# An encoder kernel's attention: one reciprocal for the first three row blocks of a head, and the last q blocks' rotation in other rounds

## The chip, the core and the metric

The kernel runs on one core of a Trainium2 chip. The core has five engines that each run their own list of instructions in order: TensorE (PE, matrix products; its weight loads are shown apart as PEld), VectorE (DVE), ScalarE (ACT), GpSimd (POOL) and SyncE (SP, which issues most transfers). An instruction that waits for another engine holds up everything behind it on its own engine. The metric is the device time of one execution in microseconds (us). Three runs of the kernel before gave 1718.39, 1720.16 and 1721.22 us, a median of 1720.16 us.

## The reference, cut to what matters

Two sequences of 512 tokens go through two layers. Layer 0 mixes tokens by a Fourier transform, layer 1 by attention; each is followed by a squared-ReLU MLP. The change is in the attention of layer 1: 8 query heads of 128, two key/value heads, a softmax over 512 keys.

```python
q = rms_norm(q, q_gain); k = rms_norm(k, k_gain)
q = axial_rope(q, ang_row, ang_col) * (HEAD_DIM ** -0.5)
k = axial_rope(k, ang_row, ang_col)
s = jnp.einsum("bqkgd,bskd->bkgqs", q_blk, k)
p = jax.nn.softmax(s, axis=-1)
o = jnp.einsum("bkgqs,bskd->bqkgd", p, v)
```

## The kernel before, in words

Every float32 operand is split into a rounded high half and a remainder, and a product is made of three matmuls (`mm3`, lines 77, 78 and 79: high by high, high by low, low by high). A split (`split`, lines 82 and 83) is a cast on ACT and then a subtraction on DVE.

The attention has 2 x 8 = 16 heads, one after the other. A head has four row blocks of 128 queries. For each, `scores` makes a 128x512 block of scores on PE, its row maximum on DVE (line 1476), the exponential with a row sum on ACT (line 1478), the reciprocal of the sum on DVE (line 1479) and the scaling of the block by it on POOL (line 1480). `transpose_p` turns a block of 128 keys of all four row blocks with four PE transposes (line 1486), so its fourth transpose needs the head's fourth scaled block. `transpose_q` does the same for q (line 1465). `values` makes the product with v.

The loop at line 1556 runs a pipeline; one pass of it is called round n here. Round n makes the scores of head n, block by block, each followed by a set of four transposes of head n-1's probabilities; then the transposes of head n+1's q; then the values of head n-1. On PE the first block of scores of the next round stands behind the values. All of this goes through a scheduler that sets the order of each engine's list when the kernel is built, from its own costs; buffers are given out in that order too: eight temporary blocks of 128x512 (tag t2) and eight PSUM banks. So a change in the code moves rows on every engine.

The query blocks of the second sequence's last two row blocks (of heads 4 to 7) are not rotated before the loop. A generator, `norm_rope`, is called one step at a time in the loop at line 1562. Its first step makes the inverse norms, with a square root on ACT, which needs another function table than the exponential. Each of its next four steps rotates one pair of heads: two scalings on ACT (line 1434), one product on POOL (line 1440), two on DVE (line 1443), one sum on POOL (line 1445). Before, the five steps stand in rounds 3, 4, 5, 6 and 7. The blocks are first needed at the end of round 11.

Two more lines are used below: line 1417 (four sums of squares on ACT, in round 0 and 2, for these norms) and line 1571 (the loads of w_o, whose splits the scheduler puts into rounds 0 and 1, lines 82 and 83 with `w` and `raw`).

Of the kernel before, what the change touches and what calls it, by code (L numbers as in the profile page):

```python
# [14 lines left out]
AF = mybir.ActivationFunctionType  # L15
ALU = mybir.AluOpType
# [6 lines left out]
NT = S // P  # L23
# [17 lines left out]
def trunk_kernel(ctx, tc, x_in, xt_in, y_out, dcos, dsin, feat, rope, gfour, gcol, grow, gfin,  # L41
                 w_four, w_nyq, w_qkv, w_o, w_up, w_row2, w_row4, w_sum2, w_sum4, w_down):
    nc = tc.nc
# [13 lines left out]
    def nm(s):  # L57
        n_[0] += 1
        return f"{s}_{n_[0]}"

    def slot(shape, dt):
        return act.tile(shape, dt, tag="u4", name=nm("u"))

    def tm(shape=(P, 512), dt=F32):
        return tmp.tile(list(shape), dt, tag="t2", name=nm("t"))

    def small(n=4):
        return sm.tile([P, n], F32, tag="s", name=nm("s"), padded_shape=[P, 8])

    def ps():  # L70
        return psp.tile([P, 512], F32, tag="ps", name=nm("ps"))
# [4 lines left out]
    def mm3(out, lh, ll, rh, rl, first, last):  # L76
        nc.tensor.matmul(out, lh, rh, start=first, stop=False)  # L77
        nc.tensor.matmul(out, lh, rl, start=False, stop=False)  # L78
        nc.tensor.matmul(out, ll, rh, start=False, stop=last)  # L79

    def split(dst_hi, dst_lo, src, eng=nc.vector):
        nc.scalar.copy(dst_hi, src)  # L82
        eng.tensor_sub(dst_lo, src, f32(dst_hi))  # L83
# [26 lines left out]
    def load_w(src, eng=nc.vector, parts=1, home=own):  # L110
        raw = load_raw(src)
        w = home()
        for i in range(parts):
            sl = slice(i * 1024 // parts, (i + 1) * 1024 // parts)
            split(w[0][:, sl], w[1][:, sl], raw[:, sl], eng)
        return w
# [1278 lines left out]
    for which, sc in (("q", HD ** -0.5), ("k", 1.0)):  # L1395
        r = slot([P, 2, NT, HD], F32)
# [7 lines left out]
    def qkv(cg, q, t, ws, k0=0, k1=KC, o=None):  # L1404
        o = ps() if o is None else o
        cols = slice(t * P, (t + 1) * P)
        for k in range(k0, k1):
            w = ws[k // 2]
            c = (k % 2) * 512
            mm3(o, hT[q][k][:, 0, cols], hT[q][k][:, 1, cols],  # L1410
                w[0][:, c : c + 512], w[1][:, c : c + 512], k == 0, k == KC - 1)
        return o

    def head_squares(raw, h0, n, ss):
        junk = tm((P, n * HD), BF16)
        for h in range(h0, h0 + n):
            nc.scalar.activation(junk[:, (h - h0) * HD : (h - h0 + 1) * HD], raw[:, h * HD : (h + 1) * HD],
                                 AF.Square, accum_out=ss[:, h : h + 1])
# [42 lines left out]
    def transpose_q(q, h):  # L1461
        pt = ps()
        c = (h % 2) * HD
        for t in range(NT):
            nc.tensor.transpose(pt[:, t * P : (t + 1) * P], qr[q, h // 2][:, t, c : c + HD], ident)
        qT = slot([P, 2, 512], F32R)
        split(qT[:, 0], qT[:, 1], pt)
        return qT

    def scores(q, h, qT, t):  # L1470
        kk = kT[q, h // 4]
        s = ps()
        cols = slice(t * P, (t + 1) * P)
        mm3(s, qT[:, 0, cols], qT[:, 1, cols], kk[:, 0], kk[:, 1], True, True)
        m, sm_ = small(1), small(1)
        nc.vector.tensor_reduce(m[:, :1], s, AX.X, ALU.max, negate=True)
        p = tm()
        nc.scalar.activation(p, s, AF.Exp, bias=m[:, :1], accum_out=sm_[:, :1])
        nc.vector.reciprocal(sm_[:, :1], sm_[:, :1])
        nc.gpsimd.tensor_scalar(p, p, sm_[:, :1], 1.0, ALU.mult, ALU.mult)  # L1480
        return p

    def transpose_p(probs, sc):
        pt = ps()
        for t in range(NT):
            nc.tensor.transpose(pt[:, t * P : (t + 1) * P], probs[t][:, sc * P : (sc + 1) * P], ident)
        k = slot([P, 2, 512], F32R)
        split(k[:, 0], k[:, 1], pt)
        return k

    def values(q, h, pts):
        o = ps()
        c = (h // 4) * HD
        for sc in range(NT):
            vh, vl = vt[q][0][:, sc, c : c + HD], vt[q][1][:, sc, c : c + HD]
            mm3(o, vh, vl, pts[sc][:, 0], pts[sc][:, 1], sc == 0, sc == NT - 1)
        t = slot([P, 2, 512], F32R)
        split(t[:, 0], t[:, 1], o)
        oT[q, h] = t
# [7 lines left out]
    for cg in (2, 0, 1):  # L1507
        ws = wkv if cg == 2 else [load_w(w_qkv[cg, u], home=own if u < 2 else lent) for u in range(4)]
        for q in range(NSEQ):
# [6 lines left out]
            for t in range(NT if (cg, q) != (1, 1) else 2):  # L1516
                if (cg, q, t) in transposes:
                    transpose_k(transposes[cg, q, t])
                if (cg, q, t) == (1, 1, 1):
                    first = transpose_q(0, 0)  # L1520
# [9 lines left out]
                r = rs[q][:, t : t + 1]  # L1530
# [13 lines left out]
    heads = [(q, h) for q in range(NSEQ) for h in range(NH)]  # L1544
    raw, ss = slot([P, 1024], F32), small(8)
    o = qkv(1, 1, 2, ws)
    probs = [scores(*heads[0], first, t) for t in range(NT)]
    nc.scalar.activation(raw[:, :512], o, AF.Copy, scale=rs[1][:, 2:3])
    head_squares(raw, 0, 4, ss)
    qT = transpose_q(*heads[1])  # L1550
# [5 lines left out]
    for n in range(1, len(heads) + 1):  # L1556
        pts, nxt = [], []
        for t in range(NT):
            if n < len(heads):
                nxt.append(scores(*heads[n], qT, t))  # L1560
            pts.append(transpose_p(probs, t))
            if n > 2 and t == 0:
                next(todo, None)
        last = nxt[-1] if nxt else last
        if n + 1 < len(heads):
            qT = transpose_q(*heads[n + 1])
        values(*heads[n - 1], pts)
        if n == 2:
            head_squares(raw, 4, 4, ss)
        probs = nxt  # L1570
        if n in (6, 8, 10, 12):
            ahead.append(load_w(w_o[len(ahead)], nc.vector, 2))
# [294 lines left out]
```

## Time and profile before

| | |
|---|---|
| median of three runs | 1720.16 us |
| the profiled execution | 1717.6 us, of which the span is 1715.8 us |
| PE busy | 99% of the span, granted clock 0.997 |
| DVE, ACT, POOL busy | 72%, 50%, 20% |
| the attention's rounds | from 853 to 985 us of the span |

A row of the timeline reads: start in us, duration in us, engine, line, operation, output tile <- input tiles, shape, count; in brackets how long the engine was idle before it, and what ended that. Matmuls overlap in the pipeline, so a matmul shows 0.39 us though the next starts 0.23 us later; a PE that is 99% busy can still lose time, and it is seen best in the distance between equal places of two rounds.

### The profile page before, as it was taken

Reading aid. Unit: us, or ns where it says so; the run is one execution under the profiler, and the core shown is the slowest. Engines: PE = TensorE matmul, PEld = TensorE weight load, DVE = VectorE, ACT = ScalarE, POOL = GpSimd, SP = SyncE. Lnnn points to the kernel's source line nnn. Section 1 sums busy time; section 2 is a strip of 40 time slices with the busy share of each in tenths; the row PEclk is TensorE's granted clock in tenths of the full one; section 3 lists DMA queues with packets and bytes.
Section 4 is the critical chain, followed back from the end, with each engine's and each line's share of the span. In section 5 each row is a group of like instructions: output and inputs, shape, how many; then the busy total and the mean of one; then the engine's idle time right before and its main releaser. Section 6 shows DMA issues by size and latency. Waiting matters only on the chain. (4 is left out here: it accounts for less than half of the span.)

```text
span 1715.8 us, 21892 instructions
## 1 busy us (share of the span) xinstructions
PE 1691.0 (99%) x7847; PEld 1395.8 (81%) x7847; DVE 1239.0 (72%) x1836; ACT 857.8 (50%) x1508; POOL 335.5 (20%) x302
## 2 busy tenths in 40 slices
PE   9999999999999999999999999999999999999997
PEld 6988887888788888888877888788788888888886
DVE  8679776456887879976588834687655479787865
ACT  6666445446343434457687714554444544344334
POOL 1321442321000000232244303114422200000004
PEclk9999999999999999999999999999999999999999
DMA  9742554449554645610000213335534686455322
GB/s 322 191 143 95 196 202 163 161 172 367 197 197 138 214 148 175 232 42 28 26 25 1 99 50 123 110 114 197 181 142 148 225 303 237 163 204 193 115 74 99
DMA packets 103679, 266.33 MB, mean 155 GB/s; under 512 B 10177, under 2 KB 10177, under 8 KB 103570
## 3 DMA queue, kind: packets, MB, share of 16 engines
q1 hardware_dynamic: 87410, 232.95, 38.4%
q10 hardware_dynamic: 14112, 25.70, 4.0%
q0 software_dynamic: 2048, 6.29, 1.8%
q8 instruction: 61, 1.00, 0.2%
q14 instruction: 48, 0.39, 0.1%
HBM read 189.93 MB, written 73.92 MB: 154 GB/s over the span
## 5 line engine op out<-in xcount | busy, mean ns | idle before, releaser
L833 PE MATMUL ps<-u,w 128*128 128x512 f32 x4656 | 1068.9, 390 | 5.3 <-DVE w L83 1.2
L833 PEld LDWEIGHTS ps<-u,w 128*128 128x128 f32 x4656 | 873.4, 188 | 192.3 <-DVE w L83 2.7
L82 ACT CAST w<-raw 128x1024 fp32r<-128x1024 f32 (+1 forms) x224 | 217.6, 981 | 435.8 <-PE ps L833 266.6
L83 DVE TENSOR_TENSOR w<-raw,w 128x1024 fp32r<-128x1024 f32 (+1 forms) x224 | 258.0, 1154 | 71.9 <-ACT w L82 71.5
L159 POOL TENSOR_TENSOR t<-t,t 128x512 f32<-128x512 f32 (+1 forms) x56 | 79.0, 1410 | 738.1 <-ACT t L157 682.0
L83 DVE TENSOR_TENSOR u<-u,u 128x1024 fp32r<-128x1024 f32 x132 | 157.6, 1220 | 25.8 <-ACT u L82 25.2
L82 ACT CAST u<-u 128x1024 fp32r<-128x1024 f32 x132 | 132.4, 1044 | 70.5 <-PE ps L833 48.5
L77 PE MATMUL ps<-u,u 128*128 128x512 f32 (+2 forms) x388 | 150.0, 388 | 1.9 <-DVE u L496 1.4
L1089 DVE TENSOR_TENSOR u<-ps,u 128x512 f32<-128x512 f32 x160 | 109.4, 686 | 53.9 <-PE ps L833 53.3
L78 PE MATMUL ps<-u,u 128*128 128x512 f32 (+2 forms) x388 | 144.8, 373 | 1.4 <-DVE u L83 1.4
L79 PE MATMUL ps<-u,u 128*128 128x512 f32 (+2 forms) x388 | 144.5, 372 | 0.0
L833 PE MATMUL ps<-u,u 128*128 128x512 f32 x576 | 138.2, 391 | 2.4 <-DVE t L924 2.3
L833 PEld LDWEIGHTS ps<-u,u 128*128 128x128 f32 x576 | 107.6, 188 | 27.1 <-DVE t L924 2.6
L950 POOL TENSOR_TENSOR u<-u 128x512 f32<-128x512 f32 x28 | 36.6, 1305 | 411.3 <-ACT u L849 411.3
L83 DVE TENSOR_TENSOR u<-ps,u 128x512 fp32r<-128x512 f32 (+4 forms) x118 | 74.6, 650 | 17.4 <-ACT u L82 16.2
L78 PEld LDWEIGHTS ps<-u,u 128*128 128x128 f32 x388 | 73.4, 189 | 14.1 <-DVE u L83 3.9
L77 PEld LDWEIGHTS ps<-u,u 128*128 128x128 f32 x388 | 73.5, 190 | 13.8 <-DVE u L496 1.6
L79 PEld LDWEIGHTS ps<-u,u 128*128 128x128 f32 x388 | 73.1, 188 | 13.0 <-DVE u L83 0.4
L911 DVE TENSOR_TENSOR t<-ps,u 128x512 f32<-128x512 f32 x30 | 20.7, 690 | 81.8 <-PE ps L833 63.8
L82 ACT CAST u<-ps 128x512 fp32r<-128x512 f32 (+4 forms) x118 | 64.6, 562 | 28.8 <-PE ps L79 10.9
L816 DVE TENSOR_TENSOR u<-ps,u 128x512 f32<-128x512 f32 (+1 forms) x48 | 30.8, 644 | 64.8 <-PE ps L79 64.8
L77 PE MATMUL ps<-u,w 128*128 128x512 f32 (+2 forms) x192 | 64.9, 338 | 0.0
(237 smaller groups left out, 2005.8 us busy)
## 6 DMA issues: line engine op xcount, KB each, us to landing
raw<-w_up SPq DMA_DIRECT2D x82, 512.0 KB, 4.5
u<-spill_t SPq DMA_DIRECT2D x60, 512.0 KB, 6.1
raw<-w_sum SPq DMA_DIRECT2D x56, 512.0 KB, 4.0
u<-spill_b SPq DMA_DIRECT2D x45, 512.0 KB, 5.2
spill_t<-u SPq DMA_DIRECT2D x87, 256.0 KB, 2.0
spill_b<-t ACTq DMA_DIRECT2D x60, 256.0 KB, 3.2
raw<-w_row SPq DMA_DIRECT2D x28, 512.0 KB, 4.1
park<-u SPq DMA_DIRECT2D x24, 512.0 KB, 3.3
```

What stands on the lines that cost most here:

```text
L77: nc.tensor.matmul(out, lh, rh, start=first, stop=False)
L78: nc.tensor.matmul(out, lh, rl, start=False, stop=False)
L79: nc.tensor.matmul(out, ll, rh, start=False, stop=last)
L82: nc.scalar.copy(dst_hi, src)
L83: eng.tensor_sub(dst_lo, src, f32(dst_hi))
L159: nc.gpsimd.tensor_add(acc[q][:, :n], acc[q][:, :n], s[:, :n])
L816: nc.vector.tensor_add(x[:, :n], o[:, :n], x[:, :n])
L833: nc.tensor.matmul(o, w[x][:, sl], h[k][y], start=first and k + i == 0, stop=k == n - 1 and i == 2, skip_group_check=not first)
L911: nc.vector.tensor_add(u2, ob, t[:, 0])
L950: eng.tensor_sub(t[:, 0], b12, b11)
L1089: nc.vector.tensor_add(x, o, x)
```

## The change

`scores` gets a list. The four row sums of a head now lie in the four columns of one small tile. Nothing is done with them after the first and the second block. After the third block one reciprocal over three columns is made, and the three scalings on POOL follow it; after the fourth block come a reciprocal of the last column and the fourth scaling. A head has two reciprocals instead of four, 32 fewer in all, and still four scalings. The generator is now called in rounds 3, 5, 7, 8 and 9.

```diff
-    def scores(q, h, qT, t):
+    def scores(q, h, qT, t, out):
...
-        m, sm_ = small(1), small(1)
+        m = small(1)
+        if t == 0:
+            out.append(small(NT))
+        r = out[0]
         nc.vector.tensor_reduce(m[:, :1], s, AX.X, ALU.max, negate=True)
         p = tm()
-        nc.scalar.activation(p, s, AF.Exp, bias=m[:, :1], accum_out=sm_[:, :1])
-        nc.vector.reciprocal(sm_[:, :1], sm_[:, :1])
-        nc.gpsimd.tensor_scalar(p, p, sm_[:, :1], 1.0, ALU.mult, ALU.mult)
-        return p
+        nc.scalar.activation(p, s, AF.Exp, bias=m[:, :1], accum_out=r[:, t : t + 1])
+        out.append(p)
+        if t > 1:
+            new = range(0, 3) if t == 2 else range(3, 4)
+            nc.vector.reciprocal(r[:, new.start : new.stop], r[:, new.start : new.stop])
+            for u in new:
+                nc.gpsimd.tensor_scalar(out[u + 1], out[u + 1], r[:, u : u + 1], 1.0, ALU.mult, ALU.mult)
...
-    probs = [scores(*heads[0], first, t) for t in range(NT)]
+    probs = []
+    for t in range(NT):
+        scores(*heads[0], first, t, probs)
...
-                nxt.append(scores(*heads[n], qT, t))
-            pts.append(transpose_p(probs, t))
-            if n > 2 and t == 0:
+                scores(*heads[n], qT, t, nxt)
+            pts.append(transpose_p(probs[1:], t))
+            if n in (3, 5, 7, 8, 9) and t == 0:
                 next(todo, None)
```

In the changed kernel the lines have other numbers: the row maximum is line 1479, the exponential 1481, the reciprocal 1485, the scaling 1487, the transposes of the probabilities 1492.

The first place is DVE's list in a round with a rotation (round 6 before, round 5 of the change), from the first row maximum on. `s` is a small tile, `ps` a PSUM bank, `u` a split block, `t` a temporary block; L83 is the subtraction of a split. Before:

```order
L1476 TENSOR_REDUCE s_1411_8039<-ps_1410_8035 128x1
L83 TENSOR_TENSOR u_1409_8032<-ps_1408_8019,u_1409_8032 128x512
L83 TENSOR_TENSOR u_1415_8051<-ps_1414_8046,u_1415_8051 128x512
L1479 RECIPROCAL s_1412_8040<-s_1412_8040 128x1
L1476 TENSOR_REDUCE s_1420_8067<-ps_1419_8063 128x1
L1443 TENSOR_TENSOR t_1418_8056<-t_1416_8054,u_913_6000 128x2x64 x2
L83 TENSOR_TENSOR u_1424_8079<-ps_1423_8074,u_1424_8079 128x512
L1476 TENSOR_REDUCE s_1426_8086<-ps_1425_8082 128x1
L1479 RECIPROCAL s_1421_8068<-s_1421_8068 128x1
L83 TENSOR_TENSOR u_1430_8098<-ps_1429_8093,u_1430_8098 128x512
L1476 TENSOR_REDUCE s_1432_8105<-ps_1431_8101 128x1
L1479 RECIPROCAL s_1427_8087<-s_1427_8087 128x1
```

And in the change:

```order
L1479 TENSOR_REDUCE s_1362_7896<-ps_1361_7892 128x1
L83 TENSOR_TENSOR u_1366_7906<-ps_1365_7901,u_1366_7906 128x512
L1479 TENSOR_REDUCE s_1371_7922<-ps_1370_7918 128x1
L1479 TENSOR_REDUCE s_1376_7938<-ps_1375_7934 128x1
L1443 TENSOR_TENSOR t_1369_7911<-t_1367_7909,u_913_6000 128x2x64 x2
L83 TENSOR_TENSOR u_1374_7931<-ps_1373_7926,u_1374_7931 128x512
L83 TENSOR_TENSOR u_1379_7951<-ps_1378_7946,u_1379_7951 128x512
L1479 TENSOR_REDUCE s_1381_7958<-ps_1380_7954 128x1
L1485 RECIPROCAL s_1363_7897<-s_1363_7897 128x3
L83 TENSOR_TENSOR u_1384_7969<-ps_1383_7964,u_1384_7969 128x512
L83 TENSOR_TENSOR u_1386_7977<-ps_1385_7972,u_1386_7977 128x512
L1485 RECIPROCAL s_1363_7897<-s_1363_7897 128x1
```

Before, the first reciprocal stands fourth; now the one for three columns stands behind all four row maxima, both rotation products and three subtractions, and the fourth column's two subtractions behind that.

The second place is DVE's list at the end of round 3, behind the last step of the inverse norms (L137). The row maxima are those of head 3's last three blocks and of head 4's first (ps_1348_7817 before, ps_1336_7797 in the change). Before:

```order
L1476 TENSOR_REDUCE s_1327_7740<-ps_1326_7736 128x1
L83 TENSOR_TENSOR u_1345_7798<-ps_1344_7793,u_1345_7798 128x512
L1476 TENSOR_REDUCE s_1333_7759<-ps_1332_7755 128x1
L1476 TENSOR_REDUCE s_1339_7778<-ps_1338_7774 128x1
L1479 RECIPROCAL s_1328_7741<-s_1328_7741 128x1
L1479 RECIPROCAL s_1334_7760<-s_1334_7760 128x1
L1476 TENSOR_REDUCE s_1349_7821<-ps_1348_7817 128x1
L83 TENSOR_TENSOR u_1347_7814<-ps_1346_7801,u_1347_7814 128x512
L1479 RECIPROCAL s_1340_7779<-s_1340_7779 128x1
```

And in the change:

```order
L1479 TENSOR_REDUCE s_1318_7723<-ps_1317_7719 128x1
L1479 TENSOR_REDUCE s_1323_7739<-ps_1322_7735 128x1
L1479 TENSOR_REDUCE s_1328_7759<-ps_1327_7755 128x1
L83 TENSOR_TENSOR u_1333_7778<-ps_1332_7773,u_1333_7778 128x512
L1479 TENSOR_REDUCE s_1337_7801<-ps_1336_7797 128x1
L1485 RECIPROCAL s_1308_7695<-s_1308_7695 128x3
L1485 RECIPROCAL s_1308_7695<-s_1308_7695 128x1
```

The remainder of head 4's q (the L83 row) has moved behind all three maxima, and the first three columns' reciprocal stands behind the first row maximum of the next head. Before, the first block's reciprocal came ahead of this whole piece; now head 3's first block is scaled with the others.

The third place is ACT's list in round 0, from the load of the exponential's table on. CAST u is the high half of a split of head 1's q (u_1256_7471 before, u_1253_7466 in the change) or of transposed probabilities, CAST w that of w_o. Before:

```order
L1478 ACT_TABLE_LOAD
L1478 ACTIVATE t_1241_7423,s_1240_7421<-ps_1238_7416,s_1239_7420 128x512
L1478 ACTIVATE t_1245_7434,s_1244_7432<-ps_1242_7427,s_1243_7431 128x512
L82 CAST u_1256_7471<-ps_1255_7466 128x512
L1478 ACTIVATE t_1249_7445,s_1248_7443<-ps_1246_7438,s_1247_7442 128x512
L82 CAST w_1561_8569<-raw_1560_8567 128x512
L1478 ACTIVATE t_1253_7456,s_1252_7454<-ps_1250_7449,s_1251_7453 128x512
L1417 ACTIVATE t_1254_7461,s_1236_7390<-u_1235_7389 128x128 x4
```

And in the change:

```order
L1481 ACT_TABLE_LOAD
L1481 ACTIVATE t_1241_7423,s_1240_7421<-ps_1238_7416,s_1239_7420 128x512
L1481 ACTIVATE t_1244_7431,s_1240_7421<-ps_1242_7425,s_1243_7429 128x512
L1481 ACTIVATE t_1247_7439,s_1240_7421<-ps_1245_7433,s_1246_7437 128x512
L1481 ACTIVATE t_1250_7451,s_1240_7421<-ps_1248_7445,s_1249_7449 128x512
L1417 ACTIVATE t_1251_7456,s_1236_7390<-u_1235_7389 128x128 x4
L82 CAST u_1253_7466<-ps_1252_7461 128x512
L82 CAST w_1528_8514<-raw_1527_8512 128x512 x2
L1560 ACTIVATE u_1235_7389<-ps_1254_7469,rs_978_6293 128x512
L82 CAST w_1580_8711<-raw_1579_8709 128x512
L82 CAST u_1260_7509<-ps_1259_7504 128x512
L82 CAST w_1580_8711<-raw_1579_8709 128x512
```

The cast of head 1's q has moved from behind two exponentials to behind four and the four sums of squares.

SP's list is the same, transfer for transfer. POOL's list has the same number of rows; in a rotated round the rotation's product and sum now stand ahead of all four scalings of that head, where before one scaling stood ahead of them.

## The prediction

> **What bounds the kernel now.** I read the page's busy times first, then the waits of the attention's stretch (853 to 990 us), then the timeline of each engine there. First the page, and from the waits the largest group that names the code of the change:
>
> ```profile
> PE 1691.0 (99%) x7847; PEld 1395.8 (81%) x7847; DVE 1239.0 (72%) x1836; ACT 857.8 (50%) x1508; POOL 335.5 (20%) x302
> ```
>
> ```profile
> PEld ps L1486 <- POOL t L1480: 3.1, 8, 1.1
> ```
>
> TensorE is the bound. In 137 us its queue waited 3.1 us, eight times, for a scaled block (at most 1.1 us at once). All that the change can win is such waiting. The timeline shows it best in the transposes of q, one set at the end of each round:
>
> ```profile
> 864.60 0.60 PE L1465 MATMUL ps<-ident,u 128*128 128x128 f32 x4
> ...
> 873.26 0.60 PE L1465 MATMUL ps<-ident,u 128*128 128x128 f32 x4
> ...
> 880.97 0.60 PE L1465 MATMUL ps<-ident,u 128*128 128x128 f32 x4
> ...
> 889.51 0.60 PE L1465 MATMUL ps<-ident,u 128*128 128x128 f32 x4
> ...
> 898.88 0.60 PE L1465 MATMUL ps<-ident,u 128*128 128x128 f32 x4
> ...
> 924.17 0.60 PE L1465 MATMUL ps<-ident,u 128*128 128x128 f32 x4
> ```
>
> The first four are the ends of rounds 1 to 4. Round 3 takes 880.97 - 873.26 = 7.71 us, and later rounds without rotation take the same: PE's own work. Over it, round 2 loses 8.66 - 7.71 = .95, round 4 .83, round 5 1.66, and rounds 6 to 8 (898.88 to 924.17, three rounds) 25.29 - 23.13 = 2.16. With .96 at the entry (below) and .4 behind the last round this is about 6.95 us, the most that could be won (.4%).
>
> **The change part by part.** A clean round first (round 11, no rotation):
>
> ```profile
> 936.51 0.68 DVE L1476 TENSOR_REDUCE s<-ps 128x1 f32<-128x512 f32 x1
> ...
> 941.10 0.17 DVE L1479 RECIPROCAL s<-s 128x1 f32<-128x1 f32 x1
> ```
>
> ```profile
> 942.69 0.69 POOL L1480 TENSOR_SCALAR t<-t,s 128x512 f32<-128x512 f32 x1 [0.56 <-DVE s L1479]
> ```
>
> ```profile
> 943.48 0.60 PE L1486 MATMUL ps<-ident,t 128*128 128x128 f32 x4
> ```
>
> Let T be the start of a round's first set of probability transposes; the next set of the next round starts at T + 7.71, here 943.48, so T = 935.77. Of the four transposes in .60 us the last starts .34 in (an estimate from the row), so the fourth scaled block is wanted at T + 8.05. It is ready at 942.69 + .69 = 943.38 = T + 7.61: .44 us to spare. With the change three scalings come in a row behind the third reciprocal. Moving up the row maxima as the changed order does, I get that reciprocal at T + 4.39 by DVE's spacings (.6 for a maximum or a subtraction, the first maximum at T + .74) and the fourth block at T + 7.5. So a clean round pays nothing: PE's 7.71 us hide it. The 32 removed reciprocals are hidden by the same cover.
>
> *The spacings in a rotated round.*
>
> ```profile
> 905.45 0.16 DVE L1479 RECIPROCAL s<-s 128x1 f32<-128x1 f32 x1
> 905.53 0.67 DVE L1476 TENSOR_REDUCE s<-ps 128x1 f32<-128x512 f32 x1
> 906.11 1.17 DVE L1443 TENSOR_TENSOR t<-t,u 128x128 f32<-128x128 f32 x2
> 907.20 0.68 DVE L83 TENSOR_TENSOR u<-ps,u 128x512 fp32r<-128x512 f32 x1
> 907.80 0.67 DVE L1476 TENSOR_REDUCE s<-ps 128x1 f32<-128x512 f32 x1
> ...
> 911.10 0.15 DVE L1479 RECIPROCAL s<-s 128x1 f32<-128x1 f32 x1
> ```
>
> ```profile
> 911.41 0.70 POOL L1480 TENSOR_SCALAR t<-t,s 128x512 f32<-128x512 f32 x1 [0.64 <-PE ps L79]
> ```
>
> From start to start a reciprocal costs DVE .08 us, a maximum or subtraction .6, the two rotation products 1.09. From a reciprocal's start to its scaling's start it is .31. The changed list of such a round (shown above) then runs: maximum T + .74, subtraction 1.34, maxima 1.94 and 2.54, products 3.14, subtractions 4.23 and 4.83, maximum 5.43, reciprocal of three columns 6.03. Four scalings of .69 follow: 6.03 + .31 + 2.76 + .05 = T + 9.15, where T + 8.05 is wanted: **1.1 us late**. Before, the first scaling stood ahead of the products and the others came one by one.
>
> Rounds 6 to 8 hold two rotations in place of three: 1.1 + 0 + 1.1 - 2.16 = **+.04**. Round 5 loses its rotation: **-1.66**. Rounds 9 and 10 were clean and now follow the rotations of rounds 8 and 9; the delayed round before shifts the lanes by about .1, so 1.0 each, **+2.0**.
>
> *Entry (rounds 0 and 1).*
>
> ```profile
> 855.92 0.69 ACT L1478 ACTIVATE t<-ps,s 128x512 f32<-128x512 f32 x1 [0.22 <-DVE s L1476]
> ...
> 857.26 0.58 ACT L82 CAST u<-ps 128x512 fp32r<-128x512 f32 x1
> ...
> 858.07 0.68 DVE L83 TENSOR_TENSOR u<-ps,u 128x512 fp32r<-128x512 f32 x1
> ...
> 859.52 0.39 PE L79 MATMUL ps<-u,u 128*128 128x512 f32 x1
> ...
> 859.58 0.33 ACT L1417 ACTIVATE t<-u 128x128 bf16<-128x128 f32 x1
> ...
> 859.75 0.49 PE L1486 MATMUL ps<-ident,t 128*128 128x128 f32 x3
> ...
> 860.75 0.62 ACT L82 CAST w<-raw 128x512 fp32r<-128x512 f32 x1
> ...
> 861.05 0.33 PE L1486 MATMUL ps<-ident,t 128*128 128x128 f32 x1 [0.82 <-POOL t L1480]
> ...
> 861.14 0.48 PE L77 MATMUL ps<-u,u 128*128 128x512 f32 x1
> ```
>
> PE's fourth transpose would follow its three at 859.75 + .34 = 860.09 and came at 861.05: .96 lost. Now ACT makes four exponentials from 855.92 (.68 apart: 858.64), the four sums of squares (860.75 - 859.58 = 1.17: 859.81) and only then head 1's q cast. Its subtraction starts .81 behind the cast's start (858.07 - 857.26) and lasts .6: 861.2, where L79, which wants it, ran at 859.52. Behind that L79 PE needs 861.14 - 859.52 - .96 = .66 us to the next L77: 861.85 against 861.14, **+.7**. The wait for the scaling is gone; the q split is late in its place.
>
> *Rounds 1 and 2.*
>
> ```profile
> 866.11 0.76 ACT L1478 ACTIVATE t<-ps,s 128x512 f32<-128x512 f32 x1
> ```
>
> ```profile
> 868.42 0.68 DVE L83 TENSOR_TENSOR w<-raw,w 128x512 fp32r<-128x512 f32 x1
> ```
>
> ```profile
> 868.60 1.05 POOL L1480 TENSOR_SCALAR t<-t,s 128x512 f32<-128x512 f32 x1 [0.56 <-DVE s L1479]
> ```
>
> ```profile
> 869.80 0.48 PE L77 MATMUL ps<-u,u 128*128 128x512 f32 x1
> ```
>
> Head 1's third exponential started 5.36 us behind the sums of squares (860.75 to 866.11). Three more casts now stand between, about .5 each, so 859.81 + 6.9 = 866.7; the reciprocal follows .8 to 1.1 later (867.6), the scalings at 867.9. One of four lies beside a w_o subtraction and costs 1.05, as the row at 868.60 does beside 868.42: ready at 867.9 + 3 x .69 + 1.05 = 871.0, and the next L77 at 871.3 where it was 869.80. Of these 1.5 us the entry holds .7: **+.8**. The Trainium skill, "SBUF — State Buffer", section "Who interferes with whom", has a VectorE instruction with two inputs in SBUF contend with a GpSimd instruction that reads SBUF; the pair 868.42 and 868.60 agrees (1.05 against .69), and without that rule the sum would be .4 less.
>
> *Round 3.* Head 2's third exponential now stands behind the cast of the fourth transposed block, whose set ends at T + 4.0. One cast (.5) and .8 to the reciprocal make T + 5.4; with .31 + 2.76 + .05 the fourth block is ready at T + 8.5 instead of 8.05: **+.4**.
>
> *Round 4 (behind the table loads of round 3).*
>
> ```profile
> 879.52 0.69 POOL L1480 TENSOR_SCALAR t<-t,s 128x512 f32<-128x512 f32 x1 [2.48 <-DVE s L131]
> ```
>
> ```profile
> 883.07 0.68 DVE L1476 TENSOR_REDUCE s<-ps 128x1 f32<-128x512 f32 x1
> ```
>
> ```profile
> 883.83 1.28 ACT L1478 ACT_TABLE_LOAD   x1 [1.35 <-DVE s L1476]
> ...
> 885.12 0.69 ACT L1478 ACTIVATE t<-ps,s 128x512 f32<-128x512 f32 x1
> ```
>
> ```profile
> 884.61 0.39 PE L79 MATMUL ps<-u,u 128*128 128x512 f32 x1
> ```
>
> Before, head 3's first block was scaled at 879.52, ahead of the loads, and PE could transpose it while the others came. Now nothing of head 3 is scaled before its third exponential, at 885.12 + .68 = 885.8. The reciprocal comes at 886.6, the scalings end at 886.6 + .31 + 2.76 = 889.7, and the first set's fourth transpose waits for that. Behind it stand two score blocks (.69 each), two sets (.45 each) and .1: the q mark comes at 892.2 against 889.51, **+2.7**. (Head 4's q subtraction, moved behind three maxima, ends at 885.5 where its L79 ran at 884.61; that lies inside the same wait.)
>
> *What the trace doesn't show* is a reciprocal of three columns.
>
> ```profile
> 881.13 0.20 DVE L133 RECIPROCAL s<-s 128x8 f32<-128x8 f32 x1 [0.90 <-ACT s L132]
> ```
>
> One column takes .15 (911.10), eight take .20. I take .16, near the one column; at .20 each of some eight paying rounds would lose .05 more, .4 us at most, and nothing suggests a gain. The end of the attention is costed at +.1: its last head's scalings also come in a row, with the values behind them.
>
> **The sum:** .7 + .8 + .4 + 2.7 - 1.66 + .04 + 2.0 + .1 = +5.1 us. The profiled execution takes 1717.6 us, so 1722.7; the median of the runs is 2.56 above the profiled one, so **1725.3**.
>
> **The rivals.** *A, not slower: the scalings are not what comes last.* If the three-column reciprocal is made by T + 4.9 even in a rotated round (4.9 + .31 + 2.76 + .05 = 8.02, just in time), such a round ends only on DVE's last subtraction, at T + 6.81 against 6.46 wanted by the same spacings: .35 each, 1.4 for four, in place of 1.66 + 2.16 before. That is -2.4 us, 1717.7. For it: PE runs ahead by one score block and may get its exponentials early, and DVE is spared .08 x 32 = 2.6 us. Against it: the changed list puts products and three subtractions ahead of that reciprocal, 6.03 and not 4.9. Here a page bears on it: the Trainium skill, "Perfetto Trace Analysis", section "Optimizing Scalar/DVE Operations", says that fewer, larger operations pay where the engine is saturated, and that breaking them up may let work finish sooner where it is not but leaves bubbles on others. DVE's 72% in the page and PE's waits for L1480 are the second case, which is the forecast; by its first half the time would be A's.
>
> *B: only the rotated rounds pay.* ACT's and PE's queues have slack that hand lanes don't see, and entry, rounds 2 to 4 come out as before: -1.66 + .04 + 2.0 = +.4, 1720.6. For it: their +4.6 comes from three long chains of estimated starts.
>
> *C: clean rounds pay too.* If the third reciprocal stays where row 941.10 has it (T + 5.33), the fourth block is ready at 5.33 + .31 + 2.76 + .05 = 8.45, .4 late in each of five clean rounds: +2.0 on top, 1727.3. The same would come of the shared small tile, if the fourth exponential's write were held for the reciprocal of the other three columns, so that the change did not do what it says; the changed lists show no such wait.
>
> **How the numbers follow.** Forecast .55 (its own range +3 to +7 us, from single terms of .4 to 1 us), A .17, B .20, C .08. A difference of 0.2%, 3.44 us, is about what a measurement of this kernel can tell from no change. Over it lie .47 of the forecast and all of C: slower .55. Below -3.44 lies the part of A where entry and round 4 win too, .10. The rest, .35, is within. The range runs from 1718.5, which takes in B with 2 us below it and leaves out the lower three quarters of A (.13), to 1728.5, which is C with the reciprocal's .4 and .8 for its single terms and leaves out some .05.
>
> **What would show it.** Right: the L79 of round 1 near 861.2 with the q subtraction as its releaser; rounds 6, 8, 9 and 10 of 8.7 to 8.8 us between q marks, rounds 5 and 7 of 7.7, and PE released by the scaling in the slow ones; round 4 of some 11 us. Wrong: rotated rounds of 8.1 us (A), round 4 of 8.5 (B), clean rounds of 8.1 (C). A fourth block that PE never waits for would make the whole chain wrong.

## The result, and the profile after

Over twelve runs each, the changed kernel takes 1724.12 us in the median (1722.49 to 1726.88) and the kernel before 1718.78 us (1713.4 to 1721.32): 1.0032 times as long, 95% interval 1.0023 to 1.0040. It is slower by 5.3 us; forecast were 1725.3 us and, against its own base of 1720.16, 5.1 us.

First the page of the changed kernel, then the waits of its attention (the same columns as before: total, times, longest):

```profile
PE 1693.7 (98%) x7847; PEld 1397.6 (81%) x7847; DVE 1234.9 (72%) x1804; ACT 856.4 (50%) x1508; POOL 335.1 (19%) x302
```

```profile
PEld ps L1492 <- POOL t L1487: 7.9, 14, 2.0
...
PE ps L77 <- ACT u L82: 1.1, 1, 1.1
...
PE ps L79 <- DVE u L83: 0.7, 1, 0.7
```

VectorE does 32 operations and 4 us less, and TensorE's queue now waits 7.9 us for scaled blocks (14 times) where it waited 3.1 (8 times). The transposes of q at the ends of rounds 1 to 5, 8 and 10:

```profile
867.15 0.60 PE L1465 MATMUL ps<-ident,u 128*128 128x128 f32 x4
...
876.36 0.60 PE L1465 MATMUL ps<-ident,u 128*128 128x128 f32 x4
...
884.54 0.60 PE L1465 MATMUL ps<-ident,u 128*128 128x128 f32 x4
...
895.83 0.60 PE L1465 MATMUL ps<-ident,u 128*128 128x128 f32 x4
...
903.56 0.60 PE L1465 MATMUL ps<-ident,u 128*128 128x128 f32 x4
...
928.39 0.60 PE L1465 MATMUL ps<-ident,u 128*128 128x128 f32 x4
...
945.21 0.60 PE L1465 MATMUL ps<-ident,u 128*128 128x128 f32 x4
```

The distances of such marks, against those of before, show each round's share. Round 1 is counted from the q transposes at the end of round 0 (853.17 before, 855.06 after), and the end from the last q mark to the first product with w_o. Their sum is called the **attention stretch**:

| us | before | after | difference | forecast |
|---|---|---|---|---|
| round 1 (entry) | 11.43 | 12.09 | +.66 | +.7 |
| round 2 | 8.66 | 9.21 | +.55 | +.8 |
| round 3 | 7.71 | 8.18 | +.47 | +.4 |
| round 4 | 8.54 | 11.29 | +2.75 | +2.7 |
| round 5 | 9.37 | 7.73 | -1.64 | -1.66 |
| rounds 6 to 8 | 25.29 | 24.83 | -.46 | +.04 |
| rounds 9 and 10 | 15.44 | 16.82 | +1.38 | +2.0 |
| rounds 11 to 14 and the end | 43.72 | 43.89 | +.17 | +.1 |
| attention stretch | 130.16 | 134.04 | +3.88 | +5.1 |

The stretch explains 3.9 of the 5.3 us. The rest has to do with the granted clock. The two profiled spans differ by 1722.1 - 1715.8 = 6.3 us, and 1.9 of that is there before the attention begins, where every engine's list is the same. By stretches of 8 us (columns: length, busy time of PE, PEld, DVE, ACT and POOL, PE's granted clock, DMA share, GB/s) the kernel before, then the changed one:

```profile
104.00:112.00 8.00, 6.96 (x30) 4.93 (x29) 5.10 (x8) 6.97 (x13) 4.57 (x4) 0.92 0.47 178
112.00:120.00 8.00, 8.00 (x32) 6.50 (x31) 3.26 (x8) 3.16 (x6) 0.00 (x0) 0.86 0.06 23
```

```profile
32.00:40.00 8.00, 6.44 (x40) 6.04 (x39) 7.61 (x10) 7.68 (x12) 1.76 (x2) 0.80 1.05 265
80.00:88.00 8.00, 8.00 (x55) 8.00 (x56) 3.56 (x12) 3.42 (x7) 0.00 (x0) 0.79 0.01 2
```

Each of these dips loses 1.7 to 1.8 us: .08 and .14 of 8 us in the kernel before, .21 of 8 us in the last row. Ahead of the attention the kernel before has one dip and the changed kernel two; in the profiles of the experiments there are none (move alone) to two (own tiles, at the same two places), in the same lists, so these dips are not of the change.

The mean granted clock of the twelve runs of the changed kernel is .9957; that of 99 runs of the kernel before, taken beside the experiments, is .9974. Over all these runs a clock lower by .001 goes with 1.2 us (a least-squares line with a level for each kernel), so .0017 is an estimated 2.1 us. Against the mean of those 99 runs the changed kernel is 5.7 us slower, so at one clock the change costs 3.6 us, near the stretch's 3.9. Whether the change lowers the clock, or met a lower one, is not settled. Three kernels below have a long wait of TensorE in round 4 as it does, and means of .9966 (joined only), .9969 (after, products on POOL) and .9960 (own tiles, late scalings); those without it have .9969 to .9982. The experiments are therefore compared by the stretch, and their times are given beside it.

### The profile page after: what moved, and what is told of

It reads as the page before. It is cut to its first block, busy times and chain, and to the rows that moved or that the text cites. A ratio compares the mean times of both kernels' runs of the same rounds, so it can differ in the third digit from the quotient of the medians.

```text
span 1722.1 us, 21882 instructions
## 1 busy us (share of the span) xinstructions
PE 1693.7 (98%) x7847; PEld 1397.6 (81%) x7847; DVE 1234.9 (72%) x1804; ACT 856.4 (50%) x1508; POOL 335.1 (19%) x302
## 5 line engine op out<-in xcount | busy, mean ns | idle before, releaser
L83 DVE TENSOR_TENSOR w<-raw,w 128x1024 fp32r<-128x1024 f32 (+1 forms) x224 | 258.0, 1154 | 68.1 <-ACT w L82 67.3
L83 DVE TENSOR_TENSOR u<-u,u 128x1024 fp32r<-128x1024 f32 x132 | 157.8, 1222 | 25.6 <-ACT u L82 25.0
L79 PE MATMUL ps<-u,u 128*128 128x512 f32 (+2 forms) x388 | 145.4, 375 | 0.7 <-DVE u L83 0.7
L83 DVE TENSOR_TENSOR u<-ps,u 128x512 fp32r<-128x512 f32 (+4 forms) x118 | 74.9, 653 | 30.9 <-ACT u L82 30.1
L79 PEld LDWEIGHTS ps<-u,u 128*128 128x128 f32 x388 | 73.8, 190 | 14.5 <-DVE u L83 2.0
```

## The experiments

Each kernel was profiled once and has ten or eleven times ("own tiles, late scalings" has four), given as a ratio to the kernel before with a 95% interval. A stretch rests on one profile; where lists agree, its pieces do to some .04 us (round 1 of the seven kernels with the old entry takes 11.39 to 11.43), unless the clock dips. All their rounds first (us; r is a round, "end" is the piece behind the last mark; rounds 11 to 14 are 7.70 to 7.73 each, but 8.38 to 8.42 with "own tiles, late scalings"):

| kernel | stretch | r1 | r2 | r3 | r4 | r5 | r6 | r7 | r8 | r9 | r10 | end |
|---|---|---|---|---|---|---|---|---|---|---|---|---|
| before | 130.16 | 11.43 | 8.66 | 7.71 | 8.54 | 9.37 | 8.46 | 8.38 | 8.45 | 7.71 | 7.73 | 12.90 |
| after | 134.04 | 12.09 | 9.21 | 8.18 | 11.29 | 7.73 | 8.56 | 7.71 | 8.56 | 8.27 | 8.55 | 13.07 |
| joined only | 133.53 | 12.05 | 9.20 | 8.15 | 12.16 | 8.07 | 8.14 | 8.24 | 8.25 | 7.70 | 7.71 | 13.03 |
| moved only | 130.44 | 11.42 | 8.67 | 7.73 | 8.55 | 8.90 | 8.60 | 7.71 | 8.29 | 8.37 | 8.47 | 12.90 |
| four, late in code | 129.94 | 11.42 | 8.63 | 7.71 | 8.55 | 8.93 | 8.35 | 7.71 | 8.38 | 8.27 | 8.26 | 12.90 |
| joined from head 4 | 131.72 | 12.08 | 8.39 | 7.71 | 9.06 | 8.33 | 9.13 | 8.16 | 8.17 | 8.25 | 8.55 | 13.04 |
| the same, own tiles | 130.93 | 11.39 | 8.66 | 7.71 | 8.57 | 8.90 | 9.00 | 8.16 | 8.17 | 8.24 | 8.23 | 13.05 |
| shared, one by one | 131.03 | 12.10 | 8.38 | 7.70 | 9.08 | 8.30 | 8.45 | 7.74 | 8.58 | 8.40 | 8.48 | 12.97 |
| own tiles, late scalings | 141.23 | 13.21 | 8.62 | 8.41 | 11.11 | 7.73 | 9.01 | 8.33 | 8.71 | 9.00 | 9.00 | 14.54 |
| all but head 3 | 132.51 | 12.10 | 9.22 | 8.17 | 8.40 | 8.90 | 9.02 | 8.16 | 8.17 | 8.23 | 8.26 | 13.05 |
| after, products on POOL | 135.25 | 12.10 | 9.17 | 8.16 | 11.26 | 7.70 | 9.03 | 7.71 | 8.98 | 8.61 | 8.65 | 13.06 |
| before, products on POOL | 130.07 | 11.39 | 8.67 | 7.73 | 8.57 | 8.99 | 7.91 | 9.04 | 8.62 | 7.70 | 7.71 | 12.91 |
| the same, moved | 130.52 | 11.41 | 8.66 | 7.71 | 8.57 | 8.90 | 8.91 | 7.71 | 8.13 | 8.71 | 8.07 | 12.91 |
| before, in place, on POOL | 130.71 | 11.40 | 8.67 | 7.70 | 8.48 | 11.97 | 7.93 | 7.70 | 7.71 | 7.71 | 7.70 | 12.91 |

### The two halves of the change

Joined only, against the changed kernel:

```diff
-            if n in (3, 5, 7, 8, 9) and t == 0:
+            if n > 2 and t == 0:
```

> The joined reciprocals alone, the rotation in rounds 3 to 7 as before. The attention stretch is taken from the q transposes at the end of round 0 to the first product with w_o: 130.16 us before, 134.04 with the whole change. Theory (a head's scalings come last, and late): the entry, rounds 2, 3 and 4 lose what they lose with the whole change (+.66, +.55, +.47, +2.75 = +4.4), round 5, which still has a rotation ahead of it, some 1.2 over 7.71 instead of 1.66 (-.4), rounds 6 to 8 .85 each (+.4), clean rounds nothing, the end +.2: +4.6, a stretch of 134.8. Rival 'the place of the rotation pays': without the move it is no slower than before, 130 to 131.

Time 1.0020 (1.0011 to 1.0029), stretch 133.53. Entry and rounds 2 to 4 came as expected but for .87 us in round 4, which is the clock. TensorE's rows there, and stretches of 2 us (columns as above):

```profile
889.34 0.47 PE L1492 MATMUL ps<-ident,t 128*128 128x128 f32 x1 [1.73 <-POOL t L1487]
889.47 0.78 PE L77 MATMUL ps<-u,u 128*128 128x512 f32 x1
```

```profile
886.00:888.00 2.00, 0.92 (x3) 0.19 (x1) 1.41 (x3) 1.99 (x6) 0.00 (x0) 1.00 0.01 4
888.00:890.00 2.00, 0.66 (x2) 0.61 (x3) 1.28 (x4) 2.00 (x7) 1.41 (x3) 0.81 0.00 0
890.00:892.00 2.00, 2.00 (x9) 1.57 (x8) 0.66 (x2) 0.49 (x2) 1.97 (x3) 0.50 0.00 0
892.00:894.00 2.00, 2.00 (x12) 1.78 (x11) 1.41 (x5) 1.59 (x4) 0.74 (x1) 0.84 0.00 0
```

After the wait of 1.73 us the clock is at .50, and from there to the q mark PE takes 5.44 us (889.34 to 894.78) where the changed kernel takes 4.57 (891.26 to 895.83) at full clock. Without that .87 the stretch is 132.66, **+2.5** over the kernel before. So the rival "the place of the rotation pays" falls as the whole cause, but the remaining 1.4 us come with the move. Rounds 6 to 8, at 8.14 to 8.25, lose .43 to .54 over 7.71, less than before, where I had expected .85 each.

Moved only, against the kernel before:

```diff
-            if n > 2 and t == 0:
+            if n in (3, 5, 7, 8, 9) and t == 0:
```

> The rotation in rounds 3, 5, 7, 8 and 9 with four separate reciprocals and early scalings. Theory: entry and rounds 2 to 4 as before, round 5 7.7 instead of 9.37 (-1.66), and four rounds (6, 8, 9, 10) of about 8.43 in place of three: +.7; in all -.9, a stretch of 129.2. Rival 'the place of the rotation pays': rounds 9 and 10 lose more than a rotated round does before (over 1 us each) and the stretch is 131 or more.

Time .9999 (.9990 to 1.0007), stretch 130.44: +.28 and not -.9. Rounds 6, 8, 9 and 10 pay what I expected, but round 5 falls only to 8.90. Of its loss .47 was the rotation's; 1.2 us stay without one. They look like a trace of round 3's table loads: from the second load (882.80) to 892.2 ScalarE works with one pause of .3 us, and in round 5 TensorE waits for its casts and for VectorE's subtractions. No run takes the loads away, so this is not shown.

### What in the joining pays: the tile, the operation or the lateness

Four reciprocals, late in the code, against the changed kernel:

```diff
-            out.append(small(NT))
+            out.append([small(1) for _ in range(NT)])
...
-            nc.vector.reciprocal(r[:, new.start : new.stop], r[:, new.start : new.stop])
             for u in new:
+                nc.vector.reciprocal(r[u][:, :1], r[u][:, :1])
...
```

> As the whole change, but with four reciprocals of one column, each on a small tile of its own; the first three still wait for the third exponential, and so do their scalings. Theory: the lateness is the cost and the operation is nothing, so the stretch is that of the whole change and up to .16 us more in each of some eight paying rounds: 134.0 to 135.3. Rival 'the joined operation pays' (the width of the operation, or the tile that four exponentials and two reciprocals share): much of the +3.88 goes, 130.5 to 132.

Time 1.0001 (.9992 to 1.0010), stretch 129.94, below even the rival's range, so by these words the rival wins. But the run did not do what I wrote of it: nothing but the code's order held the reciprocals back, and the scheduler put them where their sums are ready. VectorE in round 10 of this run, behind a rotation:

```profile
931.26 0.21 DVE L1486 RECIPROCAL s<-s 128x1 f32<-128x1 f32 x2
...
932.69 0.16 DVE L1486 RECIPROCAL s<-s 128x1 f32<-128x1 f32 x1
```

The first two blocks' reciprocals stand ahead of the third's. So the code's order alone does not delay an operation here; only its inputs do. (It is not without effect: this run's lists differ from the moved kernel's, and so do their stretches, by .5 us.) The width of the operation costs next to nothing: in the changed kernel's attention three columns take 166 ns and one takes 155 (by form):

```profile
L1485 DVE RECIPROCAL s<-s 128x3 f32<-128x3 f32 x16 | 2.7, 166 | 1.1 <-ACT t L1481 1.1
L1485 DVE RECIPROCAL s<-s 128x1 f32<-128x1 f32 x16 | 2.5, 155 | 0.9 <-ACT t L1481 0.9
```

Joined from head 4 on, heads 0 to 3 one by one on the shared tile (against the changed kernel):

```diff
-        if t > 1:
-            new = range(0, 3) if t == 2 else range(3, 4)
+        g = q * NH + h
+        late = g > 3
+        if t > 1 or not late:
+            new = range(t, t + 1) if not late or t == 3 else range(0, 3)
```

> As the whole change, but heads 0 to 3 make their reciprocals and scalings one by one. Theory: entry and rounds 2 to 4 are as before (0 instead of +4.43), the rest as with the whole change (-1.64 - .46 + 1.38 + .16 = -.56): a stretch of 129.6. Rival 'late everywhere' (the price of the rounds is carried on by the scheduler or the buffers): 131 or more.

Time 1.0005 (.9996 to 1.0014), stretch 131.72, a miss: nothing in heads 0 to 3 is late, and yet the entry takes 12.08. That made the shared tile a suspect. The same with heads 0 to 3 as before, a tile for each sum:

```diff
+        late = q * NH + h > 3
+        if late:
...
+        else:
+            m, sm_ = small(1), small(1)
...
+        if not late:
+            nc.vector.reciprocal(sm_[:, :1], sm_[:, :1])
+            nc.gpsimd.tensor_scalar(p, p, sm_[:, :1], 1.0, ALU.mult, ALU.mult)
+        elif t > 1:
```

> Joined reciprocals in heads 4 to 15 alone; heads 0 to 3 word for word as before, with a small tile for each row sum; the rotation moved. Theory: entry and rounds 2 to 5 as in the kernel with the move alone (11.42, 8.67, 7.73, 8.55, 8.9), later as with the whole change (+.2), end +.17: a stretch of 130.8. Rival: the later rounds carry the price as in the run that joined from head 4 on a shared tile, 131.7.

Time .9999 (.9990 to 1.0008), stretch 130.93, as expected in the sum and up to round 5; rounds 6 to 10 share their loss out otherwise than in the changed kernel (9.00 and 8.16 in rounds 6 and 7), which I did not look into. With the joining in heads 4 to 15 alone the change is all but free: +.49 against the move alone.

Shared tile, everything one by one, against the changed kernel:

```diff
-        if t > 1:
-            new = range(0, 3) if t == 2 else range(3, 4)
+        if True:
+            new = range(t, t + 1)
```

> The four row sums in the columns of one tile, but each reciprocal and each scaling made at once, one by one; the rotation moved. Nothing is late, only the tile is shared. Theory 'the late scalings pay': 130.4, as with the move alone. Rival 'the shared tile pays' (it moves the scheduler's order: four exponentials in a row ahead of head 1's q cast): the entry takes 12.08, round 4 9.06 as in the run that joined from head 4 on, and the stretch is 131.5 or more.

Time 1.0010 (1.0001 to 1.0020), stretch 131.03, between the two: +.59 over the move alone. Entry (12.10) and round 4 (9.08) are as the rival said. ScalarE in this run:

```profile
859.54 0.69 ACT L1481 ACTIVATE t<-ps,s 128x512 f32<-128x512 f32 x1
...
861.38 0.58 ACT L82 CAST u<-ps 128x512 fp32r<-128x512 f32 x1
```

The fourth exponential stands ahead of the sums of squares and head 1's q cast, just as in the changed kernel. So the entry's .66 us is the **tile's**: four columns of one tile change the scheduler's order, without any late reciprocal. Round 2 gives .29 back.

Late scalings without tile or joining, against the move alone (`one_` is 1, made from the third sum, so that three scalings wait for it):

```diff
+        if t == 2:
+            one_ = small(1)
+            nc.vector.tensor_scalar(one_[:, :1], sm_[:, :1], 0.0, 1.0, ALU.mult, ALU.add)
         nc.vector.reciprocal(sm_[:, :1], sm_[:, :1])
-        nc.gpsimd.tensor_scalar(p, p, sm_[:, :1], 1.0, ALU.mult, ALU.mult)
-        return p
+        out.append((p, sm_))
+        if t == 2:
+            for x, r in out:
+                nc.gpsimd.tensor_scalar(x, x, r[:, :1], one_[:, :1], ALU.mult, ALU.mult)
+        if t == 3:
+            nc.gpsimd.tensor_scalar(p, p, sm_[:, :1], 1.0, ALU.mult, ALU.mult)
...
```

> Four tiles and four reciprocals made one by one, but the scalings of the first three blocks wait for the third exponential (their second factor is a one made from the third row sum, one small VectorE operation more per head); the rotation moved. Nothing is shared or joined, only the scalings are late. Theory 'the late scalings pay': entry 11.4 to 12.1, round 2 9.2, round 3 8.2, rounds 4 and 5 together 19.0: a stretch of 133 to 134. Rival 'the shared tile pays': 130.4 to 131.

Time 1.0078 (1.0063 to 1.0093), stretch 141.23, far over what I expected: lateness pays, and here in clean rounds too (about 8.4). Round 11 of this run, VectorE, POOL and PE (T, counted back from its first set's fourth transpose, is 952.7):

```profile
958.07 0.15 DVE L1481 TENSOR_SCALAR s<-s 128x1 f32<-128x1 f32 x1
```

```profile
958.40 2.29 POOL L1486 TENSOR_SCALAR t<-t,s,s 128x512 f32<-128x512 f32 x3 [5.45 <-DVE s L1481]
```

```profile
961.41 0.33 PE L1493 MATMUL ps<-ident,t 128*128 128x128 f32 x1 [0.34 <-POOL t L1488]
```

The third sum is used 5.4 us into the round, where rival C had put it (5.33), and the block is late. (A scaling with two factors takes .76 instead of .69; that is .2 of the .7.) The changed kernel in a clean round:

```profile
953.43 0.17 DVE L1485 RECIPROCAL s<-s 128x3 f32<-128x3 f32 x1
```

```profile
949.10 0.60 PE L1492 MATMUL ps<-ident,t 128*128 128x128 f32 x4
```

4.33 us into the round, as forecast (4.39): the row maxima have moved up. It is not the shared tile that moves them. In the run with the shared tile and everything one by one, the start of a clean round and the reciprocal of its third block:

```profile
945.90 0.60 PE L1492 MATMUL ps<-ident,t 128*128 128x128 f32 x4
```

```profile
951.24 0.16 DVE L1485 RECIPROCAL s<-s 128x1 f32<-128x1 f32 x1
```

That is 5.34 us, as in the kernel before (5.33). Only where reciprocals are joined does the scheduler bring the maxima forward; so the tile costs .6 us, and the joining itself saves the clean rounds from its own lateness.

All but head 3, with head 3 as before (the diff as in the run with own tiles in heads 0 to 3, with `late = q * NH + h != 3`):

> The whole change, but head 3 as before. Theory: rounds 4 and 5 fall from 19.02 to what they take with the move alone, 17.45 (-1.57), all else stays: a stretch of 132.5. Rival 'the table loads alone set round 4': no change, 134.0.

Time 1.0011 (1.0001 to 1.0020), stretch 132.51, as expected: rounds 4 and 5 take 17.30 instead of 19.02 (rounds 6 to 10 share their loss out as in the run with own tiles, with .19 more in all). Round 4's price is that nothing of head 3 is scaled ahead of the table load. And round 5 is back at 8.90, without a rotation: round 4's wait had covered it.

### What holds the rotated rounds

The rotation's products of line 1443 on GpSimd, in the loop's generator, for the changed kernel, the one before, and that with the move:

```diff
-                nc.vector.tensor_mul(t2[:, :, sl], x[:, :, other], every(table[:, 1, t, sl]))
+                eng.tensor_mul(t2[:, :, sl], x[:, :, other], every(table[:, 1, t, sl]))
```

> The whole change, with the rotation's two products of line 1443 (those of the loop's generator alone) on GpSimd instead of VectorE. Theory (in a rotated round VectorE's chain to the third reciprocal is what comes last): rounds 6, 8, 9 and 10 fall from 8.56, 8.56, 8.27 and 8.55 to about 7.8, rounds 2 to 4 keep their price: a stretch of 131.0 against 134.04. Rival (GpSimd's row of scalings is what comes last, and the products stand ahead of it): no gain, 134 or more.

> The kernel before, with the rotation's two products of line 1443 on GpSimd. Theory: rounds 6 to 8 fall from 8.46, 8.38 and 8.45 to about 7.8, round 5 by some .4: a stretch of 127.8 against 130.16. Rival (GpSimd late): 130 or more.

> As the one before, with the rotation in rounds 3, 5, 7, 8 and 9. Theory: round 5 stays at 8.9, rounds 6, 8, 9 and 10 fall from 8.60, 8.29, 8.37 and 8.47 to about 7.8: a stretch of 128.0, so that the move is worth nothing once the products don't hold VectorE. Rival (GpSimd late): 130 or more.

Times 1.0030 (1.0021 to 1.0040), .9998 (.9989 to 1.0007) and .9998 (.9989 to 1.0006); stretches 135.25, 130.07 and 130.52: three misses. The stretches are in the rivals' ranges, but not for the rivals' reason. In the kernel before, the queue of TensorE waits in this part (895 to 950 us) more for subtractions of splits than for scalings:

```profile
PEld ps L78 <- DVE u L83: 2.2, 4, 0.7
PEld ps L1486 <- POOL t L1480: 0.6, 3, 0.2
```

In the three runs it is the same, with .5 us at most for scalings; so GpSimd's scalings are not what comes last. ScalarE in the second run, in round 7:

```profile
907.89 0.69 ACT L1478 ACTIVATE t<-ps,s 128x512 f32<-128x512 f32 x1 [1.01 <-POOL t L1443]
```

An exponential waits 1.0 us for the block it writes, one of eight, which the rotation still holds. Such waits are 2.0 us in this run (two), 3.0 and 2.9 in the first and the third (four each) and, for the products on VectorE, 1.4 in the kernel before (three). That a longer wait took the gain is a guess that the last run tests. It gives two of the rotation's three blocks back, in the kernel before, with the products on GpSimd as above:

```diff
-            x, t1, t2 = [tm((P, step, HD)) for _ in range(3)]
+            if eng is nc.vector:
+                x, t1, t2 = [tm((P, step, HD)) for _ in range(3)]
+            else:
+                x = raw[:, h0 * HD : (h0 + step) * HD].rearrange("p (h d) -> p h d", h=step)
+                t1 = outs[h0 // 2].rearrange("p (h d) -> p h d", h=2)
+                t2 = tm((P, step, HD))
...
```

> The kernel before, with the rotation's two products on GpSimd and two of its three temporary blocks gone: the scaling on ScalarE is made in place, and the first product goes into the q blocks themselves. In the run with the products on GpSimd alone an exponential waited up to 1.0 us for a block that a rotation held. Theory (that wait is what took the gain): rounds 6 to 8 fall from 8.46, 8.38 and 8.45 to 7.8 to 8.0, round 5 from 9.37 to 8.9, a stretch of 128.0 against 130.16. Rival (ScalarE's and VectorE's order in a rotated round is what costs, not the blocks): 129.5 or more.

Time .9998 (.9989 to 1.0007), stretch 130.71. Rounds 6 to 8 fall to 7.93, 7.70 and 7.71, and no exponential waits for a rotation's block any more. How much of the fall is due to that is not separated, since the rotations' first products have left these rounds too (the last starts at 896.81). And round 5 takes 11.97: with nothing to hold them the scheduler begins three of the four rotations between 884 and 893 us (POOL's first products below), a scaling comes behind them, TensorE waits for it, and the clock dips again (TensorE's rows, and a window).

```profile
884.65 0.74 POOL L1445 TENSOR_TENSOR u<-u,u 128x256 f32<-128x256 f32 x1 [3.75 <-ACT u L1439]
...
889.48 0.74 POOL L1445 TENSOR_TENSOR u<-u,u 128x256 f32<-128x256 f32 x1
...
892.20 0.73 POOL L1445 TENSOR_TENSOR u<-u,u 128x256 f32<-128x256 f32 x1
```

```profile
891.62 0.66 PE L1491 MATMUL ps<-ident,t 128*128 128x128 f32 x4 [1.22 <-POOL t L1485]
...
894.01 0.63 PE L77 MATMUL ps<-u,u 128*128 128x512 f32 x1
894.44 0.63 PE L78 MATMUL ps<-u,u 128*128 128x512 f32 x1
```

```profile
892.00:898.00 6.00, 5.75 (x20) 4.20 (x19) 3.90 (x8) 4.45 (x12) 4.13 (x8) 0.72 0.00 0
```

Matmuls that start .43 apart instead of .23 are at about half clock. No kernel tried is faster than the kernel before by more than its interval.

## Why the prediction was right, and where it was not

**The sum.** 5.1 us were forecast in the attention, and 3.88 are there. That the time still came out at +5.3 us, and within 1.2 us of the forecast, is in part luck: 1.5 to 2 us of lower clock, which I had not reckoned with, made up for rounds 6 to 10. Rival A fell with the rotated rounds, where the scalings do come last (.56 to .85 us late), and rival B with rounds 1 to 4 (+4.43).

**Round 4** (+2.7, measured +2.75) was right with its mechanism: with head 3 as before it goes away. **Rounds 2 and 3** (+.8 and +.4, measured +.55 and +.47) were right. Before round 3 the reciprocal of three columns starts at T + 5.39 and the last scaling ends at T + 8.45 (forecast 5.4 and 8.5). The four scalings of round 2, one of them beside a w_o subtraction, take 3.14 us, as reckoned (4 x .69 + .36):

```profile
869.61 3.14 POOL L1487 TENSOR_SCALAR t<-t,s 128x512 f32<-128x512 f32 x4 [6.63 <-DVE s L1485]
```

**Clean rounds** pay nothing, as forecast: the last scaling ends at T + 7.4 (7.5). Rival C is what happens where the maxima don't move up.

**The entry** (+.7, measured +.66) had the right size and place. ScalarE's cast of head 1's q ends the wait:

```profile
862.25 0.50 PE L77 MATMUL ps<-u,u 128*128 128x512 f32 x1 [1.13 <-ACT u L82]
```

L79 comes at 862.97, right behind the subtraction that starts at 862.23; less the 1.89 us by which this profile starts the attention later, that is 861.1, the sign I had named (861.2). But "now ACT makes four exponentials" is not what lateness does; the shared tile alone does it.

**Round 5** (-1.66, measured -1.64) was right by accident. The step that failed is "round 5 loses its rotation": that is worth .47. The other 1.2 went because TensorE's long wait in round 4 let the other engines catch up; with head 3 scaled early, round 5 is back at 8.90. Against the move alone, joining costs 19.02 - 17.45 = 1.57 us in rounds 4 and 5 together, not 2.75.

**Rounds 6 to 10** (+2.04, measured +.92) had the right chain and a term that was too large. The step is "the two rotation products 1.09". In the changed kernel's four slow rounds the products start at T + 3.13 to 3.15 (forecast 3.14), but the reciprocal of three columns at T + 5.84, 5.84, 5.50 and 5.51 (6.03), and the rounds pay .85, .85, .56 and .84 (1.1 and 1.0). The pair of products between takes .97, .97, .65 and .64 us, where the row of before (906.11) takes 1.17. POOL beside that row, then pairs of the changed kernel (the first and the third) with POOL's product beside each:

```profile
905.70 0.69 POOL L1480 TENSOR_SCALAR t<-t,s 128x512 f32<-128x512 f32 x1 [1.98 <-DVE s L1479]
906.36 0.77 POOL L1440 TENSOR_TENSOR t<-t,u 128x256 f32<-128x256 f32 x1
```

```profile
902.85 0.97 DVE L1443 TENSOR_TENSOR t<-t,u 128x128 f32<-128x128 f32 x2
...
927.63 0.65 DVE L1443 TENSOR_TENSOR t<-t,u 128x128 f32<-128x128 f32 x2
```

```profile
902.73 0.75 POOL L1440 TENSOR_TENSOR t<-t,u 128x256 f32<-128x256 f32 x1 [3.02 <-issue]
...
927.20 0.74 POOL L1440 TENSOR_TENSOR t<-t,u 128x256 f32<-128x256 f32 x1 [2.41 <-ACT t L1434]
```

The row of before has POOL busy beside it for 1.05 us, with the end of a scaling (.28) and the rotation's product (.77). With the scalings late POOL is free there: .65 us with .31 beside it, .97 with .63. The collision that I charged in round 2 I overlooked in the row that I took as a price. Round 10 is dear in spite of its short pair, for another reason: its first scaling starts .62 us behind the reciprocal, where the other three take .26 to .33.

```profile
938.26 0.16 DVE L1485 RECIPROCAL s<-s 128x3 f32<-128x3 f32 x1
```

```profile
938.88 2.70 POOL L1487 TENSOR_SCALAR t<-t,s 128x512 f32<-128x512 f32 x4 [1.46 <-DVE s L1485]
```

The profile names the reciprocal as what it waited for, but that had ended .46 us before; what held it is open.

**The 32 reciprocals** were worth nothing, as forecast. Taken apart, 3.88 = .28 (move) + .59 (tile) + 3.01 (joined, so late). The 3.01 lie in round 2 (+.83 against the shared tile alone), round 3 (+.48) and rounds 4 and 5 (+1.64), three places where the kernel before scaled a head's first block early; the other rounds differ by .13 or less. Joined alone costs 2.5, and the move costs 1.38 on top of it though .28 by itself. The rounds say where: with the joining, rounds 5 to 8 gain .14 from having a rotation less in place of 1.16 (round 4 has taken their loss already), and rounds 9 and 10 pay 1.4 in both cases. Three joined rotated rounds in a row cost .43 to .54 each and the spaced ones .85, .85, .56 and .84. The pairs of products agree: .59 to .64 us there, .97 in the first two here and .65 in the third; in the fourth it is the late first scaling. How the scheduler comes to lay the products beside POOL's was not tried.

## What to carry to other kernels

Joining small operations of an engine that is not the bound saved nothing here, and it delays the first result to the last input. Look for the places where an early result was used early (a table load, a crowded round): there the delay was paid, and clean rounds stayed free only because the last input came earlier too. Read what pays next when a wait goes. When a time is taken from a trace row, look at what ran beside it, since the change may take that away. The scheduler here went by what an operation reads and by the tile it shares, and the place in the code alone did not hold an operation back. Where single microseconds matter, compare stretches between fixed marks, and look at the granted clock before comparing times.

## What was not expected of the hardware

A TensorE wait of 1.2 to 1.7 us can be followed by some 3.4 us at about half clock: .50 after 1.73 us in the joined kernel, whose windows lose 1.70 us in all, and .72 over 892 to 898, 1.68 us lost, after 1.22 us in the last one. The changed kernel had the same wait of 1.73 us in the same place at full clock in its profile, and the run with own tiles and late scalings a longer one, also at 1.00 in the windows around it:

```profile
891.91 0.33 PE L1493 MATMUL ps<-ident,t 128*128 128x128 f32 x1 [2.62 <-POOL t L1486]
```

So such a wait does not always bring a dip. The Trainium skill, "TensorE: Matmul & The Clock Gate", section "What's actually happening", gives half rate after an idle window of about 3.4 us that runs freely; the half rate agrees, the waits here were shorter, with .7 us of another wait close before the 1.73.

A pair of 128x2x64 products on VectorE took .48 us in the joined kernel with POOL all but idle beside it (.02 us of it):

```profile
891.95 0.48 DVE L1443 TENSOR_TENSOR t<-t,u 128x128 f32<-128x128 f32 x2
```

In the changed kernel it took .64 with .29 us of POOL's work beside it and .97 with .63, in the kernel before 1.17 with 1.05. From these four, a microsecond beside POOL's elementwise work costs an estimated .7 more.
